# First loads of a normalization kernel split by even and odd partitions over two DMA queues

## The chip, the cores and the metric

The kernel runs on one core of one Trainium2 chip; the other cores are idle. The metric is the device time of one launch in microseconds (us). Comparisons are made with runs of the kernel before that were interleaved on the same chip. A program on one core can also have a run that is more than 1.5% above the fastest of the same kernel; such a run is called slow and is left out of the comparisons.

## The reference

```python
def reference(x, gamma):              # x: (4, 8, 16, 256, 256) f32, gamma: (8, 16) f32
    B, G, C_per_g, H, W = x.shape
    mu = x.mean(axis=(3, 4), keepdims=True)
    var = ((x - mu) ** 2).mean(axis=(3, 4), keepdims=True)
    x_norm = (x - mu) / np.sqrt(var + 1e-5)
    out = x_norm * gamma[None, :, :, None, None]
    return out.astype(np.float32)
```

Each of the 512 planes of 256 x 256 numbers is normalized by its own mean and variance and multiplied by one gamma. The input and the output are 134.22 MB each.

## The kernel before

The data are cut into 32 units of 4 MB. A unit is a tile of 128 partitions x 8192 f32, so one partition holds one row of 32 KB, and eight partitions hold one plane. Six tiles ("slots") are in SBUF. A unit is loaded, its sums are taken, it is normalized in place and stored; then the slot is loaded again.

```python
    AHEAD = 6
    slots = [data.tile([P, F], F32, name=f"xt{i}") for i in range(AHEAD)]

    def load(u, queue):
        queue.dma_start(out=slots[u % AHEAD][:], in_=xv[u])

    g_row = singles.tile([1, G * C], F32, name="g_row")
    for u in range(AHEAD):
        if u == 1:
            nc.scalar.dma_start(out=g_row[:], in_=gv[None, :])
        load(u, nc.scalar if u in (1, 3) else nc.sync)
    # ... constants, and gamma spread over the partitions ...
    for u in range(U):
        t = slots[u % AHEAD]
        nc.vector.reduce_sum(out=st[:, u, 0:1], in_=t[:], axis=AX.X)
        square = nc.scalar.activation(out=junk[:], in_=t[:], func=ACTF.Square, accum_out=st[:, u, 1:2])
        # ... matmul averages over 8 partitions; root, reciprocal, times gamma: scale ...
        nc.vector.tensor_scalar(out=t[:], in0=t[:], scalar1=ps[:, 0:1], scalar2=scale[:, u : u + 1],
                                op0=ALU.add, op1=ALU.mult)
        nc.scalar.dma_start(out=ov[u], in_=t[:])
        if u + AHEAD < U:
            load(u + AHEAD, nc.sync)
```

There are two DMA queues: that of SyncE (SP, shown as q1) takes loads only; that of ScalarE (ACT, shown as q10) takes units 1 and 3, gamma, and all stores. Both run on the same 16 DMA engines (each transfer leaves 16 completion packets in the trace, one for each engine). Below, "ring" is the line of transfers that wait in a queue. With gamma's row that makes 65 transfers. They use eight DMA semaphores in turn, so the last transfer, the 65th, is on the first semaphore again.

## Time and profile before

| | before |
|---|---|
| median, in the rounds with the changed kernel | 627.1 us (626.81 to 627.21, 4 runs) |
| span of the profiled run | 625.2 us |
| busiest compute engine | VectorE, 71% |
| two DMA queues together | 99.6% of the time of 16 engines |
| rows of 32 KB for each DMA engine | 512, at 1.21 us |

First the bytes moved, from the page: the span in 40 equal slices of 15.6 us.

```profile
GB/s 369 436 417 424 434 436 436 436 436 437 434 436 434 426 426 430 434 436 436 436 434 434 436 434 434 430 426 430 434 436 436 436 432 434 436 436 434 426 426 365
```

The rate stays between 426 and 437 but for the first slice, which holds the start, slices 3 and 4, in which the first store begins, and the last slice. Next come lines from the timeline: start in us, length in us, engine, line, operation; in brackets the idle time before and what ended it. They are the first reduce, and the issues of the first and second store.

```profile
20.32 8.69 DVE L103 TENSOR_REDUCE st<-xt 128x1 f32<-128x8192 f32 x1 [13.70 <-DMA xt<-in_x_dram]
...
35.38 0.35 ACTq L130 DMA_DIRECT2D out_dram<-xt  x1
...
50.30 0.35 ACTq L130 DMA_DIRECT2D out_dram<-xt  x1
```

VectorE starts on unit 0 only at 20.32 us, when the whole of it has landed. The change is aimed at this wait and at the following lines, the closing waits of SyncE (line view in the stretch 624.05 to 624.3 us: count, shortest/median/longest in ns, first start and last end in us):

```profile
L158 SPq EVENT_SEMAPHORE  x4: 28/28/38760, 585.3 to 624.2; - x4
L158 SPq DRAIN  x1: 7/7/7, 624.3 to 624.3; - x1
```

One wait of 38,760 ns holds the last landing, and three short ones stand behind it, ahead of the drain.

### The profile page before, as it was taken

How to read it: one execution, taken by the hardware profiler on the slowest of the kernel's cores; microseconds unless marked ns; L12 is line 12 of the kernel's file. 1: busy time of each engine (PE TensorE's matmuls, PEld its weight loads, DVE VectorE, ACT ScalarE, POOL GpSimd, SP SyncE). 2: the span in 40 equal slices, each digit the busy share in tenths (PEclk: the TensorE clock that was granted, in tenths of full speed). 3: DMA queues.
4: the chain of work that ended last, by engine and by line, in shares of the span. 5: the costliest groups of instructions: out<-in, count | busy, mean ns of one | idle time of the engine just before them, and what ended most of it. 6: DMA issues, size and time to landing. Idle time of an engine off the chain costs nothing.

```text
span 625.2 us, 626 instructions
## 1 busy us (share of the span) xinstructions
PE 21.4 (3%) x80; PEld 19.5 (3%) x80; DVE 443.2 (71%) x162; ACT 238.8 (38%) x98; POOL 1.3 (0%) x9
## 2 busy tenths in 40 slices
PE   2000000000000000000000000000000000000000
PEld 2000000000000000000000000000000000000000
DVE  0699999998867668676687766776667867668620
ACT  0444444444444224443244432344423443224400
POOL 0000000000000000000000000000000000000000
DMA  8999999999999999999999999999999999999998
GB/s 369 436 417 424 434 436 436 436 436 437 434 436 434 426 426 430 434 436 436 436 434 434 436 434 434 430 426 430 434 436 436 436 432 434 436 436 434 426 426 365
DMA packets 9220, 268.46 MB, mean 429 GB/s; under 512 B 1025, under 2 KB 1026, under 8 KB 1026
## 3 DMA queue, kind: packets, MB, share of 16 engines
q10 hardware_dynamic: 4898, 142.61, 52.8%
q1 hardware_dynamic: 4320, 125.83, 46.8%
q14 instruction: 2, 0.02, 0.0%
HBM read 134.22 MB, written 134.22 MB: 429 GB/s over the span
## 4 chain that ended last, share of the span: by engine, by line
another core or an unknown queue 64%; DMA 16%; DVE 13%; SPq 1%; PE 1%; issue 0%; ACT 0%
DMA xt<-in_x_dram 9%; DVE st L103 8%; DMA out_dram<-xt 7%; DVE xt L126 4%; SPq L48 1%; PE ps L112 1%; ACT std L117 0%; DVE nvar L113 0%; DVE rstd L121 0%; DVE scale L123 0%
## 5 line engine op out<-in xcount | busy, mean ns | idle before, releaser
L103 DVE TENSOR_REDUCE st<-xt 128x1 f32<-128x8192 f32 x32 | 277.9, 8684 | 111.2 <-DMA xt<-in_x_dram 111.2
L104 ACT ACTIVATE junk<-xt 128x8192 uint8<-128x8192 f32 x32 | 225.0, 7030 | 272.2 <-DMA xt<-in_x_dram 229.0
L126 DVE TENSOR_SCALAR xt<-xt,ps,scale 128x8192 f32<-128x8192 f32 x32 | 145.6, 4550 | 1.2
L117 ACT ACTIVATE std<-nvar,eps_t 128x1 f32<-128x1 f32 x32 | 9.4, 294 | 79.6 <-DVE nvar L113 79.6
L112 PE MATMUL ps<-st,navg 128*128 128x2 f32 x64 | 17.9, 349 | 568.0 <-DVE st L103 568.0
L112 PEld LDWEIGHTS ps<-st,navg 128*128 128x128 f32 x64 | 16.0, 312 | 569.8 <-issue 569.8
L113 DVE TENSOR_SCALAR nvar<-ps 128x1 f32<-128x1 f32 x32 | 9.2, 287 | 23.8 <-PE ps L112 23.8
L121 DVE RECIPROCAL rstd<-std 128x1 f32<-128x1 f32 x32 | 5.3, 164 | 11.6 <-ACT std L117 11.6
L104 ACT ACTIVATION_READ_ACCUMULATOR junk<-xt 128x1 f32 x32 | 6.0, 186 | 0.0
L123 DVE TENSOR_TENSOR scale<-rstd,g_col 128x1 f32<-128x1 f32 x32 | 5.1, 159 | 1.1
L84 PE MATMUL g_ps<-one,g_rep 1*128 1x1 f32 x16 | 3.5, 346 | 2.9 <-DVE g_rep L79 2.9
L84 PEld LDWEIGHTS g_ps<-one,g_rep 1*128 1x128 f32 x16 | 3.5, 325 | 2.9 <-POOL navg L68 2.9
L90 DVE COPY g_col<-g_ps 128x8 f32<-128x8 f32 x1 | 0.2, 166 | 3.7 <-PE g_ps L84 3.7
L74 ACT ACT_TABLE_LOAD x1 | 1.3, 1283 | 2.2 <-issue 2.2
L79 DVE COPY g_rep<-g_row 1x1024 f32<-1x1024 f32 x1 | 0.7, 681 | 2.1 <-DMA g_row<-in_gamma_dram 2.1
L64 POOL TENSOR_SCALAR_AFFINE_SELECT navg<-navg 128x128 f32<-128x128 f32 x1 | 0.4, 403 | 0.1
L68 POOL TENSOR_SCALAR_AFFINE_SELECT navg<-navg 128x128 f32<-128x128 f32 x1 | 0.4, 398 | 0.1
L63 POOL MEMSET navg<- 128x128 f32 x1 | 0.2, 220 | 0.0
L74 ACT ACTIVATE root_eps<-eps_t 128x1 f32<-128x1 f32 x1 | 0.2, 203 | 0.0
L147 POOL MEMSET const-bfloat16-1.0<- 128x1 bf16 x1 | 0.1, 101 | 0.0
L147 POOL MEMSET const-uint8-127<- 128x1 uint8 x1 | 0.1, 101 | 0.0
L147 POOL MEMSET const-float32-0.0<- 128x1 f32 x1 | 0.1, 98 | 0.3 <-issue 0.3
(3 smaller groups left out, 0.3 us busy)
## 6 DMA issues: line engine op xcount, KB each, us to landing
out_dram<-xt ACTq DMA_DIRECT2D x32, 4096.0 KB, 67.1
xt<-in_x_dram SPq DMA_DIRECT2D x30, 4096.0 KB, 33.8
xt<-in_x_dram ACTq DMA_DIRECT2D x2, 4096.0 KB, 33.3
g_row<-in_gamma_dram ACTq DMA_DIRECT2D x1, 0.5 KB
```

Of the source, the lines that this page charges most:

```text
L48: queue.dma_start(out=slots[u % AHEAD][:], in_=xv[u])
L74: nc.scalar.activation(out=root_eps[:], in_=eps_t[:], func=ACTF.Sqrt)
L79: nc.vector.tensor_copy(out=g_rep[:], in_=g_row[:].rearrange("o (n k) -> o n k", n=NG).unsqueeze(3).to_broadcast([1, NG, K, S]),)
L84: nc.tensor.matmul(out=g_ps[:, n : n + 1], lhsT=g_rep[:, n].rearrange("o k s -> o (k s)"), rhs=one[:], start=True, stop=True,)
L103: nc.vector.reduce_sum(out=st[:, u, 0:1], in_=t[:], axis=AX.X)
L104: square = nc.scalar.activation(out=junk[:], in_=t[:], func=ACTF.Square, accum_out=st[:, u, 1:2],)
L112: nc.tensor.matmul(out=ps[:], lhsT=navg_w, rhs=st[:, u], start=True, stop=True)
L113: nc.vector.tensor_scalar(out=nvar[:, u : u + 1], in0=ps[:, 0:1], scalar1=ps[:, 0:1], scalar2=ps[:, 1:2], op0=ALU.mult, op1=ALU.add,)
L117: nc.scalar.activation(out=std[:, u : u + 1], in_=nvar[:, u : u + 1], func=ACTF.Sqrt, bias=eps_t[:], scale=-1.0,)
L121: nc.vector.reciprocal(out=rstd[:, u : u + 1], in_=std[:, u : u + 1])
L123: nc.vector.tensor_mul(out=scale[:, u : u + 1], in0=rstd[:, u : u + 1], in1=g_col[:, g : g + 1],)
L126: nc.vector.tensor_scalar(out=t[:], in0=t[:], scalar1=ps[:, 0:1], scalar2=scale[:, u : u + 1], op0=ALU.add, op1=ALU.mult,)
```

## The change

The intent, as the diff reads, is to give VectorE its first unit earlier, by loading unit 0 through both queues at once, in half-tiles of every second partition, which by the formula for the SBUF ports (cited in the prediction) still reach all 16 ports. Units 1 to 6 are split as well, which makes 72 transfers, a multiple of eight, so that the last store is on the eighth semaphore, the last that the closing waits look at.

```diff
@@ -44,15 +44,23 @@
-    def load(u, queue):
-        queue.dma_start(out=slots[u % AHEAD][:], in_=xv[u])
+    def load(u, queue, rows=slice(None)):
+        queue.dma_start(out=slots[u % AHEAD][rows], in_=xv[u, rows])
+
+    even, odd = slice(0, P, 2), slice(1, P, 2)
 
 
     g_row = singles.tile([1, G * C], F32, name="g_row")
-    for u in range(AHEAD):
-        if u == 1:
-            nc.scalar.dma_start(out=g_row[:], in_=gv[None, :])
-        load(u, nc.scalar if u in (1, 3) else nc.sync)
+    load(0, nc.sync, even)
+    nc.scalar.dma_start(out=g_row[:], in_=gv[None, :])
+    load(0, nc.scalar, odd)
+    load(2, nc.sync, even)
+    for rows in (even, odd):
+        load(1, nc.scalar, rows)
+    load(2, nc.scalar, odd)
+    for u in range(3, AHEAD):
+        for rows in (even, odd):
+            load(u, nc.sync, rows)
@@ -129,7 +137,9 @@
         nc.scalar.dma_start(out=ov[u], in_=t[:])
         if u + AHEAD < U:
-            load(u + AHEAD, nc.sync)
+
+            for rows in (even, odd) if u == 0 else (slice(None),):
+                load(u + AHEAD, nc.sync, rows)
```

## The prediction

> **What bounds the kernel now.** I read the page first: its busy slices, its DMA queues, its groups, then the chain, then stretches of time.
>
> ```profile
> span 625.2 us, 626 instructions
> ...
> DVE  0699999998867668676687766776667867668620
> ACT  0444444444444224443244432344423443224400
> ...
> DMA  8999999999999999999999999999999999999998
> ...
> q10 hardware_dynamic: 4898, 142.61, 52.8%
> q1 hardware_dynamic: 4320, 125.83, 46.8%
> ...
> L103 DVE TENSOR_REDUCE st<-xt 128x1 f32<-128x8192 f32 x32 | 277.9, 8684 | 111.2 <-DMA xt<-in_x_dram 111.2
> ```
>
> The reader is to see that no compute engine is full (VectorE is the busiest at 71%, and it waits for loads), while the DMA row is full from the first slice to the last. The two queues together took 52.8 + 46.8 = 99.6% of the time of 16 engines. The data are 134.22 MB in and 134.22 MB out, in rows of 32 KB (one partition of a tile): 2 x 4096 rows, 512 for each DMA engine. 0.996 x 625.2 us / 512 = 1.216 us a row, which is the whole span. So the kernel is 512 row times, plus what stands before the first and after the last row.
>
> The chain of waits, in the middle, says the same:
>
> ```profile
> 161.81 0.33 SPq L48
> 162.14 18.96 another core or an unknown queue
> 181.09 0.02 SPq L48
> ...
> 181.15 0.33 SPq L48
> 181.47 18.96 another core or an unknown queue
> ```
>
> The load queue issues one load each 181.15 - 161.81 = 19.34 us. In that time one load and one store move, 8.39 MB, which is 434 GB/s; 16 rows an engine, 1.21 us each. One unit of compute is shorter: from its reduce at 20.32 to its store's issue at 35.38 is 15.06 us. Stretches of time (each row: stretch, its length, busy time of the engines, clock, DMA share, GB/s) show where the rate is missed:
>
> ```profile
> 21.36:40.72 19.36, 0.56 (x2) 0.50 (x2) 18.18 (x6) 11.32 (x4) 0.00 (x0) 1.00 1.00 433
> 40.72:60.08 19.36, 1.11 (x4) 1.00 (x4) 17.25 (x7) 9.74 (x6) 0.00 (x0) 1.00 0.98 408
> ...
> 300.00:319.36 19.36, 0.56 (x2) 0.50 (x2) 13.85 (x6) 7.42 (x3) 0.00 (x0) 1.00 1.00 433
> ```
>
> Steady pace is 433 already in the stretch in which only loads run (21 to 41 us), so loads alone are no faster and no slower than loads beside stores. One stretch is short: (433 - 408) / 433 x 19.36 = 1.1 us by this count, about 0.6 us of it real, since whole rows are counted where they fall. It is where the first store's rows begin to move. The rest is the ends: the first row starts about 1.8 us into the span, and the last rows end between 622 and 624 us, after which the last landing is seen and the program closes down by 625.2 us. Nothing else is lost.
>
> ```profile
> SPq L158 <- DMA out_dram<-xt: 41.1, 1, 41.1
> ```
>
> This line (the load queue's own waits) is the closing wait on line 158: a list of waits for the eight DMA semaphores, two at a time. The last store is there on the first semaphore, which the third of these waits names. Looked at by its times, that wait starts at 585.3 us and takes 38,760 ns, to 624.06 us, and three more waits come behind it before the closing drain at 624.3 us.
>
> **What the skill says.** DMA: Bandwidth & Descriptors, section "Issuing engines are not separate DMA queues": transfers issued by different engines run on the same 16 DMA engines and interleave, so issuing from two saves sequencer time only. The trace agrees: 433 GB/s while the scalar queue carries loads and while it carries stores. Same page, "Queues, rings and completion order": an engine goes round-robin between the queues that have work, at packet granularity. The trace agrees: unit 0 on one queue and unit 1 on the other land at 20.3 and 25.2 us, although 4 MB alone is 9.7 us at 433 GB/s. Same page, "Rules for kernel authors": two transfers to disjoint partition halves are not worth it, as they serialize on the same engines. SBUF — State Buffer, section "Door 1: The DMA port swizzle": 64 neighbouring partitions reach only 8 of 16 ports; by the formula given there even partitions alone, and odd ones alone, reach all 16. No transfer of 64 partitions is in the trace of before, so neither is tested by it.
>
> **The change, part by part.**
>
> *Bytes and rows.* The same 8192 rows of 32 KB; a transfer of 64 rows gives 4 rows to each of 16 engines if it spreads over all of them. Seven more transfers add seven semaphore writes to each engine, 4-byte packets. The 64 before cost nothing that can be seen: 16 rows fill the whole 19.36 us period including two such writes. So 0.
>
> *Unit 0 over both queues.* The queue of loads has a lead of three rows (u1 lands 4.9 us after u0, four row times, in an alternation that alone would give one). The fourth row of the scalar queue is then the tenth of the engine, and ends near 2.7 + 10 x 1.21 = 14.8 us, landing at 15.4 us. Unit 0 is ready 4.9 us earlier, and its store is issued at 30.5 us in place of 35.38. But the scalar queue carries the same 8 MB of loads as before (half 0, 1, half 2 for 1 and 3), until about 44 us, and the store's rows stand behind them in that ring. So the store's data start at 44 us and land at 64 us as before, and the load that waits for this store is issued as before.
>
> *Unit 1.* It now lies behind half of unit 0: its last row is the twelfth of the scalar queue, the 26th of the engine, 2.7 + 26 x 1.21 = 34.2 us, landing at 34.8 in place of 25.2. VectorE, done with unit 0 at 30.5, waits 4.3 us. The store of unit 1 comes at 34.8 + 15.06 = 49.9, before at 50.30. The gain on the compute side is 0.4 us by then, and stores still queue in a ring that is full. Worth 0.
>
> *New waits.* There are eight semaphores; the ninth transfer must wait until the first on its semaphore has landed. In the built program the second half of unit 2 waits for gamma's row (landed by 2.1 us), the halves of 4 and 5 for those of 0, 1 and 3, the first store for a half of unit 2, which lands near 24 us. The load ring holds three more halves, 6 MB, when the first of these waits ends, so no engine runs dry. 0 on the path.
>
> *First issue.* The first load takes 0.37 us to issue for 128 rows. A 64-row one could take less or more; every shift of the first row shifts the end, as nothing later has slack. The spread of issue times in the trace is 0.33 to 0.53 us, so I put this at +0.1, give or take 0.2 us.
>
> *Closing waits.* With 72 transfers the last store is on the eighth semaphore, which the last of the waits names. Three waits at about 0.06 us each stood behind the landing, from 624.06 to the drain at 624.29; all but one step goes: -0.12 us.
>
> Sum: 627.14 + 0 + 0.1 - 0.12 = 627.1 us. What the earlier start wins is on VectorE, which has 29% idle time.
>
> **The rivals.** (1) Halves collide on the SBUF ports. If an engine takes four neighbouring rows of a half, it writes two ports in turn, and two engines may write the same port at once while another rests. The seven split units are 7 x 8 = 56 rows an engine; at up to twice 1.21 us a row that is up to +68 us, 695 us. For it: 433 GB/s is the same for reads from and writes to HBM, as a limit on the SBUF side would have it. Against: engines need not march in step, and someone who needs 72 transfers would hardly pick splits that cost 10 us each. A partial collision of 10% would be +7 us. Together some 8%. (2) The ring runs dry: if a half lands later than I think, the new waits hold up the load queue at about 40 us. A hole of one row is 1.2 us an engine. The 6 MB in the ring speak against it; 628 to 630 us. (3) The start gains: the small loss at the first store (0.6 us) or the slow first row goes away when stores begin behind another mix of loads. 626.3 us. Nothing in the profile says that it must.
>
> **Range and chances.** The repeats of before lie within 0.16 us, so the range is that of the model: a few tenths either way for the start, the first store and which engine ends last, and some more above for small collisions or a dry ring: 626.2 to 628.4 us. Faster by over 2% would need 614.6 us; 512 rows at 1.21 us are 620 us, before start and end: 1%. Slower by over 2% (639.7 us) takes rival 1: 6%. The same: 93%.
>
> **What would show it.** Right: DMA queues again at 99 to 100% of the span, 433 GB/s in the stretch from 21 to 41 us, in which only halves and whole loads run; first reduce near 15 us, first store's issue near 30 us, second store's issue within 1 us of 50; load issues 19.34 us apart from 162 us on; the closing wait followed by one step to the drain. Wrong: below 430 GB/s before 41 us (ports), a stretch between 40 and 80 us with a DMA share clearly under that of before (dry ring), or a first row well away from 1.8 us.

## The result, and the profile after

| | before | after |
|---|---|---|
| median of 4 runs each | 627.1 us (626.81 to 627.21) | 628.0 us (627.63 to 628.14) |
| ratio | | 1.0014, interval 0.9997 to 1.0032 |
| span of the profiled run | 625.2 us | 626.0 us |
| first reduce starts | 20.32 us | 15.77 us |
| last store seen landed | 624.04 us | 625.06 us |

A ratio is the mean time of one kernel's fast runs over that of the other's fast runs of the same rounds, so it is not quite the ratio of the medians quoted beside it. The verdict is "the same" (within 2%): 0.9 us longer by the medians. The same file was run again later (below): ratio 1.002, interval 1.0008 to 1.0032, and all five of its runs took longer than all eleven of the kernel before. So the small loss is real, though this first comparison alone would not show it.

These are the page's lines for the changed kernel: the span, busy tenths and GB/s in 40 slices, the two DMA queues, the reduce on VectorE, and the half-tile loads with their median time from issue to landing.

```profile
span 626.0 us, 646 instructions
...
DVE  0869999988676687666776767867668676686730
...
DMA  8999999999999999999999999999999999999998
GB/s 369 436 402 435 435 436 435 433 432 431 429 426 431 433 435 435 433 435 435 435 431 435 433 433 431 431 427 431 433 435 433 433 435 435 433 435 435 433 433 345
...
q10 hardware_dynamic: 4930, 142.61, 52.8%
q1 hardware_dynamic: 4400, 125.83, 46.8%
...
L111 DVE TENSOR_REDUCE st<-xt 128x1 f32<-128x8192 f32 x32 | 277.9, 8684 | 114.7 <-DMA xt<-in_x_dram 114.7
...
xt<-in_x_dram SPq DMA_DIRECT2D x10, 2048.0 KB, 37.1
xt<-in_x_dram ACTq DMA_DIRECT2D x4, 2048.0 KB, 23.4
```

The two queues take the same share as before, so there is no hole of note between the rows. VectorE's total wait for loads is not shorter, 114.7 us in place of 111.2. The bytes differ in the third slice (402 in place of 417) and in the last (345 in place of 365). That is where to look.

What was meant to happen did happen. From the timeline of the changed kernel: the first reduce, the first store's issue, the second reduce, the second store's issue.

```profile
15.77 8.69 DVE L111 TENSOR_REDUCE st<-xt 128x1 f32<-128x8192 f32 x1 [9.16 <-DMA xt<-in_x_dram]
...
30.83 0.39 ACTq L138 DMA_DIRECT2D out_dram<-xt  x1
...
35.19 8.69 DVE L111 TENSOR_REDUCE st<-xt 128x1 f32<-128x8192 f32 x1 [4.39 <-DMA xt<-in_x_dram]
...
50.25 0.34 ACTq L138 DMA_DIRECT2D out_dram<-xt  x1
```

Unit 0 is ready 4.55 us earlier and its store is issued as much earlier. Unit 1 pays for it: VectorE waits 4.39 us for it, and by the second store the lead is 0.05 us. Even the first store has its lead in the ring only: its data land at 63.8 us, before at 64.4 us. The stretches of time that the prediction showed for before read in the changed kernel (length, busy time of the engines, clock, DMA share, GB/s):

```profile
21.36:40.72 19.36, 0.56 (x2) 0.50 (x2) 13.79 (x6) 7.36 (x4) 0.00 (x0) 1.00 1.00 433
40.72:60.08 19.36, 1.11 (x4) 1.00 (x4) 17.20 (x7) 9.21 (x6) 0.00 (x0) 1.00 0.99 408
300.00:319.36 19.36, 0.56 (x2) 0.50 (x2) 13.88 (x6) 7.44 (x4) 0.00 (x0) 1.00 1.00 433
```

The rates are 433, 408 and 433, as before: this count of whole rows is too coarse to show what moved. The chain of waits shows the steady pace, one load issue each 179.42 - 160.08 = 19.34 us:

```profile
160.08 0.33 SPq L48
160.41 18.96 another core or an unknown queue
...
179.42 0.33 SPq L48
```

The closing waits of SyncE after (line view, 615.5 to 625.3 us) are shorter, as meant: one short wait, then the drain.

```profile
L168 SPq EVENT_SEMAPHORE  x1: 28/28/28, 625.1 to 625.1; - x1
L168 SPq DRAIN  x2: 7/7/7, 625.1 to 625.2; - x2
```

SyncE's own waits (total us, times, longest us) hold the new ones: four waits of a load's issue for an earlier load.

```profile
SPq L48 <- DMA xt<-in_x_dram: 25.3, 4, 9.2
```

They lie where the ring is full, and cost nothing that the DMA share would show.

So where is the time lost? The first place is the first instruction. In the view of the tile, in the first 1.1 us, this is the issue of the first load (length in ns, then start in us), first before and then after:

```profile
L48 SPq DMA_DIRECT2D xt<-in_x_dram x1: 371/371/371, 0.8 to 0.8; - x1
```

```profile
L48 SPq DMA_DIRECT2D xt<-in_x_dram x1: 562/562/562, 0.8 to 0.8; - x1
```

The issue of 64 alternate partitions takes 0.19 us longer than that of all 128. The DMA view of the stretch 1.5 to 3.5 us, in slices of 0.05 us, shows the first rows start; again before, then after:

```profile
DMA  0000009990999000000900090000000000000000
```

```profile
DMA  0000000000000999909009000900909009000000
```

The first row starts in the slice at 1.80 us before and at 2.15 us after.

The second place is the first store. In the DMA view of 40 to 47 us, in slices of 0.175 us, 16 rows start about together, then nothing until they are through 1.21 us (7 slices) later. Before, then after:

```profile
DMA  9994004999000499900009990000000499000089
```

```profile
DMA  0099800009940005995000009999500000499400
```

Before, two row times from the group at the 14th slice to that at the 32nd take 18 slices in place of 14. After, from the 16th to the 35th, they take 19. I call this delay the stumble: the rows of the first store begin here, and the engines lose time once. In the row records of 30 to 60 us it is rows of the load queue that grow longer: 21 of them before and 32 after take over 1.27 us, up to 1.93 and 2.00 us, in place of 1.213; no store row does.

The third place is the end. In the DMA view of 619 to 627 us, in slices of 0.2 us, digits mark where rows start (the single digit far right is no row). Before, then after:

```profile
DMA  3970903970903990900000000000000000020000
```

```profile
DMA  3039997039997039993333000000000000000200
```

Before, the last rows start in the slice at 622.2 us, in tight groups. After, the groups are drawn out, and a few engines (the row of 3s) start their last rows as late as 623.2 us. All the data are moved when the last engine is through, not the mean one.

From the starts and ends of all rows in the two traces this account can be worked out. It splits the growth of the span, 626.03 - 625.17 = 0.86 us:

| term | before | after | difference |
|---|---|---|---|
| mean end of the engines' first row | 3.93 us | 4.23 us | +0.30 |
| delay at the first store's rows (the stumble) | 0.62 us | 0.86 us | +0.23 |
| everything else until the mean end of the last rows (623.06, 623.70 us) | | | +0.11 |
| last engine behind the mean one at its last row | 0.52 us | 0.91 us | +0.38 |
| from the last row's end to the landing that the program sees | 0.46 us | 0.45 us | -0.01 |
| from that landing to the end of the span | 1.13 us | 0.97 us | -0.16 |

The figures are rounded; the sum is +0.85 us.

When does the last engine fall behind? The completion packets of the transfers tell. Before, the last engine is 0.22 us behind the mean until 136 us, 0.58 us at 175 us and 0.52 us at the end. After, it is 0.28 us behind at 101 us, when the last half-tile has landed, 0.69 us at 140 us, 0.61 us at 411 us and 0.90 us at the end. The step in the middle comes with an instruction fetch, which the page of both kernels counts:

```profile
q14 instruction: 2, 0.02, 0.0%
```

The first of the two, a packet of 8 KB, runs at 155.8 us before and at 126.1 us after, for 0.31 us, and a data row that starts as it ends takes 1.56 us and 1.75 us in place of 1.213. The rest of the lag after, some 0.3 us, comes from 411 us on, when every transfer is whole. So little of the lag arose while the half-tiles ran: 0.06 us more than before, and 0.20 us in the second profile (e12, 0.42 us at 101 us).

### The profile page after: what moved, and what is told of

Its sections match the earlier page's. It is cut to its first block, busy times and chain, and to the rows that moved or that the text cites. A ratio compares the mean times of both kernels' runs of the same rounds, so it can differ in the third digit from the quotient of the medians.

```text
span 626.0 us, 646 instructions
## 1 busy us (share of the span) xinstructions
PE 21.4 (3%) x80; PEld 19.5 (3%) x80; DVE 443.4 (71%) x162; ACT 238.8 (38%) x98; POOL 1.3 (0%) x9
## 4 chain that ended last, share of the span: by engine, by line
another core or an unknown queue 64%; DMA 19%; DVE 9%; issue 2%; SPq 1%; PE 0%; ACTq 0%; ACT 0%; DVEq 0%
DMA xt<-in_x_dram 11%; DMA out_dram<-xt 7%; DVE st L111 7%; DVE xt L134 1%; SPq L48 1%; PE ps L120 0%; ACT std L125 0%; DVE nvar L121 0%; ACTq L48 0%; DVE rstd L129 0%; DVE scale L131 0%; ACTq L55 0%; DVEq L111 0%
## 5 line engine op out<-in xcount | busy, mean ns | idle before, releaser
L111 DVE TENSOR_REDUCE st<-xt 128x1 f32<-128x8192 f32 x32 | 277.9, 8684 | 114.7 <-DMA xt<-in_x_dram 114.7
```

## The experiments

Twelve kernels ran, each beside runs of the kernel before on the same chip (medians of it: 627.0, 627.01 and 626.77 us). All gave correct results. "Spread" below is how far the last of the 16 engines is behind the first at one and the same transfer, worked out from the times at which the engines' parts of it land in the trace; it was 0.9 us at the end of the kernel before and 1.35 us at the end of the changed one. Theories to be told apart: that the loss is in the first half-tile's issue; that the ports of SBUF collide; that transfers in halves make the DMA engines fall out of step.

### The first issue: whole, halves, columns

**e1_first_whole**: the change with unit 0 whole on one queue; unit 7 is split in its place, so that there are 72 transfers again.

```diff
-    load(0, nc.sync, even)
+    load(0, nc.sync)
     nc.scalar.dma_start(out=g_row[:], in_=gv[None, :])
-    load(0, nc.scalar, odd)
...
-            for rows in (even, odd) if u == 0 else (slice(None),):
+            for rows in (even, odd) if u in (0, 1) else (slice(None),):
```

> The change, but unit 0 is loaded whole by the load queue, and unit 7 is split in its place, so that there are still 72 transfers and the last store is on the eighth semaphore. Start theory (the first issue of a half takes 0.56 us where a whole tile took 0.37, and the first row comes 0.3 us later): issue back at 0.37 us, first row back at 1.8 us, time about 0.3 us under the change, 627.7 us. First-store theory (most of the loss is a larger stumble at 42 to 46 us, where the first store's rows meet halves in the load ring): first row back, but the stumble stays and the time stays within 0.1 us of the change. If both are real: 627.7 us with the larger stumble still there.

Measured: fast runs from 627.16 to 631.47 us, one slow run of 640.07; ratio 1.005 (1.0031 to 1.007). The expected start came, as the view of the tile and the DMA view of 1.5 to 3.5 us show for this kernel:

```profile
L48 SPq DMA_DIRECT2D xt<-in_x_dram x1: 378/378/378, 0.8 to 0.8; - x1
```

```profile
DMA  0000009999990090000090900009000000000000
```

The expected time did not. In the profiled run (629.65 us) the spread is 0.6 us at the start, 2.75 us at 114 us, about when the split loads of unit 7 go by, and 4.3 us at 577 us; that last growth falls in a stretch of whole loads. One engine ends late. This was not in any theory when the run was sent, and it made the spread the second question.

**e3_first_halves**: the kernel before with unit 0 alone in two halves, both on SyncE's queue (66 transfers).

```diff
-        load(u, nc.scalar if u in (1, 3) else nc.sync)
+        for rows in (even, odd) if u == 0 else (slice(None),):
+            load(u, nc.scalar if u in (1, 3) else nc.sync, rows)
```

> The kernel before, with unit 0 alone split by even and odd partitions, both halves on the load queue: 66 transfers, last store on the second semaphore. Start theory: first issue 0.56 us, first row near 2.15 us, 0.3 us slower than before, 627.4 us. If the later first row of the change came from the order of the two queues and not from the half: first row stays at 1.8 us and the time at 627.1 us.

Measured: 627.4 us (627.3 to 627.97), ratio 1.001 (0.9998 to 1.0023), so 0.4 us above before, as expected. Issue and first rows (same two views):

```profile
L48 SPq DMA_DIRECT2D xt<-in_x_dram x1: 557/557/557, 0.8 to 0.8; - x1
```

```profile
DMA  0000000000009999999000900900000090000000
```

Both stand where the changed kernel has them. With 378 ns in e1 this shows that the longer issue belongs to the half-tile of 64 partitions and to nothing else in the change. The same view of e4 below reads 560 ns, so it is the number of 64 partitions and not their being alternate.

**e5_columns**: the change with halves by columns: all 128 partitions, 16 KB of each row.

```diff
-        queue.dma_start(out=slots[u % AHEAD][rows], in_=xv[u, rows])
+        queue.dma_start(out=slots[u % AHEAD][:, rows], in_=xv[u, :, rows])
 
-    even, odd = slice(0, P, 2), slice(1, P, 2)
+    even, odd = slice(0, F // 2), slice(F // 2, F)
```

> The change, with its halves cut by columns (all 128 partitions, 16 KB of each row) in place of partitions: the same order, queues and 72 transfers, but rows of half the size. Start theory in its narrow form (a transfer of 64 partitions is slower to issue): issue back near 0.37 us, first row near 1.8 us. If any half is slower to issue: 0.56 us again. Port theory (rows of partition halves collide when engines are out of step): no collision here, last slice of the page back at 365 GB/s, time 626.9 to 627.1 us with the closing gain of 0.15 us. If smaller rows cost by themselves, 112 rows of 16 KB an engine at even 20 ns each would add 2 us.

Measured: 627.79 us (627.37 to 628.13), ratio 1.0011 (0.9998 to 1.0023); 0.7 to 0.9 us above what was expected. The issue is short again (0.37 us) and the first row starts at 1.80 us, but the stumble is about 1 us and the spread 1.1 us. So half a tile by itself is not slow to issue; half the partitions are. The larger stumble costs some 0.3 us of the gain. The smaller rows cost more: a row of 16 KB took 0.611 us (median, 60 to 120 us), two of them 9 ns more than one row of 32 KB, which over 56 row pairs an engine is an estimated 0.5 us.

### The ports

**e4_blocks**: the change with halves of neighbouring partitions, 0 to 63 and 64 to 127.

```diff
-    even, odd = slice(0, P, 2), slice(1, P, 2)
+    even, odd = slice(0, P // 2), slice(P // 2, P)
```

> The change, with halves of neighbouring partitions (0 to 63 and 64 to 127) in place of even and odd ones. Port theory of the skill's table (64 neighbouring partitions reach 8 of 16 ports): each half runs at about half the rate where no transfer of the other half is beside it, so the seven split units cost up to 56 rows of 1.21 us an engine, 68 us more, some 640 to 695 us, and reduce of unit 0 starts later than 15 us. If the spread over engines alone decides: within 0.3 us of the change, 628.0 us.

Measured: 687.48 us (684.83 to 690.86), ratio 1.0968 (1.0941 to 1.0994). The page:

```profile
span 683.1 us, 646 instructions
...
DMA  9999999999999999999999999999999999999997
GB/s 203 203 209 213 215 292 313 363 413 437 430 430 432 436 434 434 432 430 437 432 432 432 439 434 434 430 432 436 432 430 434 437 434 436 430 434 434 432 430 305
```

The engines are as busy as ever, but rows take 2.39 to 2.58 us (20 to 85 us) and the rate is halved for five slices of 17.1 us. The Trainium skill's page SBUF — State Buffer, section "Door 1: The DMA port swizzle", gives 64 neighbouring partitions 8 of the 16 ports; the same page's section "Can I just issue two DMAs to hit both halves?" says that two transfers at once do not make up for it. Both agree with 203 to 215 GB/s here, while half-tiles were under way on two queues. The even and odd halves of the changed kernel kept 433 GB/s. A loss of the size that the first rival of the prediction gave (+68 us at most) is thus real for blocks of neighbours, and the change's way of cutting avoids it.

### Halves in the middle of the run

**e2_mid_halves**: the kernel before with units 12 to 18 split, in place of units 0 to 6 (72 transfers). It leaves the start alone.

```diff
-            load(u + AHEAD, nc.sync)
+            for rows in (even, odd) if 12 <= u + AHEAD < 19 else (slice(None),):
+                load(u + AHEAD, nc.sync, rows)
```

> The kernel before, with the loads of units 12 to 18 alone split by even and odd partitions, in mid-run, so that there are 72 transfers and the last store is on the eighth semaphore, while start and first store are as before. If halves cost nothing in themselves: first row at 1.8 us, stumble as before, closing 0.12 to 0.16 us shorter, 627.0 us. Port theory (rows of halves are slower): rate in the stretch of the split loads under 433 GB/s, up to several us more. A mid-run fee of 0.1 us, as the change shows over its first 100 us, would just cancel the closing gain: 627.1 us.

Measured: 632.82 us (632.72 to 635.68), ratio 1.0107 (1.0092 to 1.0122). It was expected to cost nothing, and cost 5.8 us. The page of the run:

```profile
GB/s 368 432 430 432 432 432 432 432 432 433 432 432 432 432 432 431 432 428 430 395 434 432 434 432 432 432 432 434 441 432 432 432 438 432 434 432 432 436 432 251
```

The last slice is at 251 where before had 365: some engines are done while others still work. The spread is 0.81 us at 200 us, when the split loads begin, 5.3 us at 363 us, soon after the last of them, and 5.4 us from there to the end: it grows while they run. The row records show how. From 195 to 370 us 88 rows, of loads and of stores, took over 1.27 us, up to 2.59 us in place of 1.213, 28 us in all; in the kernel before only 2 of the 6911 rows after 100 us did.

**e8_all_halves**: all units of the kernel before split by even and odd.

```diff
-        load(u, nc.scalar if u in (1, 3) else nc.sync)
+        for rows in (even, odd):
+            load(u, nc.scalar if u in (1, 3) else nc.sync, rows)
...
-            load(u + AHEAD, nc.sync)
+            for rows in (even, odd):
+                load(u + AHEAD, nc.sync, rows)
```

> The kernel before, with the loads of all units split by even and odd partitions. Seven split units in mid-run cost 5.8 us. Mixture theory (rows collide only while some engines write rows of a half and others those of a whole tile): little mixing here, time under 629 us. Out-of-step theory (a half's rows collide whenever engines are out of step): engines fall apart further the longer it lasts, 32 split units cost 10 us or more, and the last slice of the page falls well under 250 GB/s.

Measured: 654.35 us (653.85 to 658.09), ratio 1.0447 (1.0423 to 1.0472). The page:

```profile
DMA  9999999999999999999999999999999999999666
GB/s 377 421 415 439 423 443 417 443 415 401 434 429 432 427 431 417 429 425 423 425 429 409 421 423 423 419 411 411 431 419 405 420 395 424 405 405 401 292 278 264
```

In the last three slices the DMA share is 6 tenths: a part of the engines has nothing left. The spread stays under 0.5 us up to 101 us and grows to 38 us by 525 us. After 100 us 508 rows took over 1.27 us, up to 3.0 us. So a mixture of whole and half loads (a theory after e1 and e2) is not needed; halves alone do it, and the more of them the more.

**e9_skew_before** and **e10_skew_change**: four extra transfers, into a tile that nobody reads, put one engine about 5 us behind the others from the start, in the kernel before and in the changed one. They ask whether being out of step is itself what costs.

```diff
+    skew = singles.tile([P, 480], F32, name="skew")
+    for i in range(4):
+        r = slice(17 * i, 17 * i + 17)
+        (nc.sync, nc.scalar)[i % 2].dma_start(out=skew[r], in_=xv[U - 1, r, :480])
```

> The kernel before, with four small transfers of 17 rows of 1920 B each put ahead of all others, two on each of the two queues, into a tile that nothing reads. 17 rows go to one DMA engine alone, so one engine starts some 130 KB behind the others, about 5 us at its pace, and has that much more to do. Whole tiles only. Out-of-step theory: an engine behind the others does no harm beyond its own extra work where all transfers are whole: 5 to 6 us more, 632 to 633 us. If being out of step harms whole tiles too: 637 us or more.

> The change with the same four small transfers ahead of all others. Out-of-step theory: the engine that is behind now runs through the split units out of step, its rows collide with those of others, and the time grows by clearly more than in the kernel before: 5 us of its own and at least 3 us more, 636 us or over. If halves do no harm by being out of step, and what cost 5.8 us in mid-run was something else there (the mix with stores, the waits for semaphores): the same 5 to 6 us as in the kernel before, 633 to 634 us.

Measured: e9 631.4 us (631.16 to 632.22), ratio 1.0076 (1.0061 to 1.0091); e10 635.81 us (634.4 to 638.28), ratio 1.0147 (1.0129 to 1.0164). The lines of bytes, first e9, then e10:

```profile
GB/s 333 427 433 433 433 433 433 433 433 432 433 433 432 431 435 435 435 433 433 433 433 433 433 433 433 433 433 433 433 433 433 433 433 433 433 433 433 433 433 281
```

```profile
GB/s 329 432 430 430 430 430 428 430 437 432 434 441 432 430 430 432 432 430 438 432 434 440 432 430 430 432 432 432 434 436 432 440 434 430 430 432 430 432 430 182
```

In e9, with whole loads, the spread of the stores' queue stays at 6.25 us from 33 to 575 us: the engine that is behind stays as far behind and costs that time once, as the flat 433 shows. In e10 it is 7.7 us at first, 8.8 at 111 us, when the last half-tile has landed, 10.6 from 229 us on, and the last slice falls to 182. The difference of the two medians is 4.4 us, of which the change itself accounts for 0.9 to 1.4. So the same small transfers cost more in the changed kernel. Not shown is that the half-tiles do it alone, since most of the growth falls after them, among whole loads.

**e11_mid_columns**: e2 with halves by columns, each of which covers all partitions.

```diff
-        queue.dma_start(out=slots[u % AHEAD][rows], in_=xv[u, rows])
+        queue.dma_start(out=slots[u % AHEAD][:, cols], in_=xv[u, :, cols])
...
-            for rows in (even, odd) if 12 <= u + AHEAD < 19 else (slice(None),):
-                load(u + AHEAD, nc.sync, rows)
+            for cols in (left, right) if 12 <= u + AHEAD < 19 else (slice(None),):
+                load(u + AHEAD, nc.sync, cols)
```

> The run with units 12 to 18 split in mid-run, with the halves cut by columns in place of partitions: the same 72 transfers, waits and order, but every row of every transfer goes to the port that it goes to in a whole tile. Port theory: no engine falls behind, 626.8 to 627.3 us. If splitting in itself (more transfers, more semaphore waits, slower supply of descriptors) made engines fall behind: near 632 us as with partition halves.

Measured: the fast runs took 630.35 to 636.6 us, ratio 1.0089 (1.0059 to 1.0119); two of six were slow (645.34, which is the profiled one, and 651.58). Its profile is thus of a slow run, and only the growth of the spread is read from it: 1.0 us at 210 us, 3.4 at 225, 8 at 350 us, when the split loads are through, up to 18 later. Column halves touch every partition just as a whole load does, yet here too an engine falls behind, and the fast runs, of which there is no profile, are 0.9% longer. Collisions that come of which partitions an engine writes (my explanation of e2 at that point) are therefore not needed for the loss. The columns also halve the rows to 16 KB, so this run does not tell whether partition halves lose time for the same reason. Why a split load in mid-run makes single rows longer and drives the engines apart is left open.

### Smaller ones

**e6_gamma_pool**: the kernel before with gamma's row issued by GpSimd, which leaves 64 transfers on the two queues, so that the closing gain comes alone.

```diff
-            nc.scalar.dma_start(out=g_row[:], in_=gv[None, :])
+            nc.gpsimd.dma_start(out=g_row[:], in_=gv[None, :])
```

> The kernel before, with gamma's row loaded through the Pool queue: nothing split, and 64 transfers on the eight semaphores, so that the last store is on the eighth. If the closing gain is what it seems (three waits behind the landing become one): closing 0.15 us shorter, 626.85 us. If the Pool's transfer brings a wait of its own at the close or a later start: 627.0 us or more.

Measured: 627.21 us (626.72 to 627.43), ratio 1.0 (0.9987 to 1.0014). The closing is shorter (last landing seen at 624.73, drain at 624.81 us), but the spread of this run is 1.5 us (it jumps from 0.53 to 1.66 at about 160 us, where an instruction fetch stands at 156.4 us), and no gain is seen. Its last engine ends 1.08 us behind the mean, more than in the changed kernel, though no load is split.

**e7_sync_only**: the kernel before with all loads on SyncE's queue. It asks whether the stumble comes of stores that stand behind loads in ScalarE's ring.

```diff
-        load(u, nc.scalar if u in (1, 3) else nc.sync)
+        load(u, nc.sync)
```

> The kernel before, with all loads on the load queue, so that the first store stands behind no load in its own queue: reduce of unit 0 starts near 12 us and the first store's rows move from 27 us on. If the stumble is the price of the first store's rows whenever they come: a stretch short by some 0.6 us, now near 27 us instead of 44, time 627.0 us. If it is the price of a queue that turns from loads to stores: no stumble, 626.4 us.

Measured: 627.54 us (627.27 to 629.41), ratio 1.0013 (1.0 to 1.0026). The first reduce is at 13.2 us and the first store is issued at 28.25. The stumble moves forward with the store, to between 33 and 45 us, and it is larger, about 1.3 us. So it belongs to the first store's rows, wherever they come, and an even earlier first store gains nothing either. Its profiled run is the slowest of the five (629.41 us): the spread grows from 0.6 us at 23 us to 4.7 us at 94 us and is 3.0 us at the end. Here too no load is split, so whole loads can drive the engines apart as well, around the first stores.

**e12_change_again**: the change, without any edit. It asks whether the late last engine of the first profile was chance.

> The change once more, unedited, for a second profile. Systematic parts should come back: first issue 0.56 us, first row near 2.15 us, closing 0.15 us shorter than before. The part that I take for chance, how far the last engine ends behind the mean of all (0.4 us worse in the first profile), may differ: 627.4 to 628.2 us.

Measured: 628.13 us (628.0 to 628.2, 5 runs), ratio 1.002 (1.0008 to 1.0032). The first issue and the DMA view of 619 to 627 us:

```profile
L48 SPq DMA_DIRECT2D xt<-in_x_dram x1: 551/551/551, 0.8 to 0.8; - x1
```

```profile
DMA  9037999037999037999030300000000000000300
```

The issue is long again, and again a few engines start their last rows late, here up to 623.4 us. The spread is 1.43 us at the end, the closing 0.97 us. By the completion packets the last engine is 0.56 us behind the mean at 411 us and 0.91 us at the end, so the late growth comes again. The loss of the changed kernel thus repeats in its terms. Of the kernel before there is one profile only, and e6, with whole loads alone, has a later last engine; how much of the difference in this term is the change's is therefore not shown.

None of the twelve was faster than the kernel before, and no version that beats both came out of them. A start with the first load whole and later halves (e1) would save some 0.3 us (an estimate from the mean end of the first row) and loses more where its spread grows.

## Why the prediction was right or wrong

**What bounds the kernel: right.** The two queues' share is the same after as before to the tenth of a per cent, and no run in which compute began earlier (the change, e7) was faster than before.

**Unit 0 earlier, worth nothing: right.** Predicted 15.4 us for the first reduce and 30.5 for the first store's issue; seen 15.77 and 30.83. The difference is the late first row, below. Landing of this store: 64 us predicted, 63.8 seen.

**Unit 1 later, worth nothing: right.** Predicted 34.8 us for its landing and 49.9 for its store; seen 35.1 and 50.25.

**New waits, worth nothing: right.** SyncE has four of them, and the rows go on without a hole.

**Closing, -0.12 us: right.** It was -0.16 us in the change, and e12 has the same closing.

**First issue, +0.1: the mechanism was right, and the size was off.** It measured +0.30 us at the mean first row, at the edge of the give-or-take of 0.2. The first row at 2.15 us is also one of the signs that the prediction had named as wrong ("well away from 1.8 us"). I had taken the spread of issue times of whole tiles for that of half tiles; e3, e4 and e12 show 0.55 to 0.56 us for 64 partitions, and e1 and e5 0.37 to 0.38 for 128.

**First store, 0: mis-sized.** The third rival took up "the small loss at the first store (0.6 us)" and supposed that it might go away. It grew by 0.23 us. It varies with the mix of loads that the store meets (0.62 before, 0.75 in e3, about 1.0 in e5, about 1.3 in e7), and what makes rows longer there is open.

**"Which engine ends last": the missing term.** The prediction named it only as a part of the range, "a few tenths either way", and left it out of the sum. It is +0.38 us, the largest term, and the changed kernel's late engine came back in e12. That split loads in mid-run drive engines apart, by single rows that take longer, is shown by e2 and e8. That they did so in the change is not shown: when its last half-tile has landed, at 101 us, the last engine is 0.28 us behind the mean (0.42 in e12), before 0.22. Both kernels then step up at an instruction fetch, and the changed one gains its further 0.3 us from 411 us on, among whole loads; why is open.

**The rivals.** A loss at the ports (1) did not show in the change, and e4 shows what another cut costs: 60 us against +68 at most. The ring did not run dry (2). The start gained nothing (3). The measured 628.0 us is in the range of 626.2 to 628.4, at its upper part; the 0.9 us above the predicted 627.1 is the three terms above, 0.20 + 0.23 + 0.38 us beyond what was put down for them, with 0.1 us of other delay. That the earlier start would win nothing was foreseen with its reason; the direction of these small terms was not.

## What to carry to other kernels

Where the DMA engines are full from end to end, as here, an earlier start of compute is worth nothing: only the first row's start, delays of the rows between, the last engine's last row and the closing can move the time, so look at these four by their rows. Keep loads whole in the steady part of such a kernel: splitting seven of 32 loads there cost 5.8 us and splitting all of them 27 us, while the number of bytes and the digits of the DMA share in the middle looked as before. If a tile must be cut, do not cut it into partitions 0 to 63 and 64 to 127 (60 us here, against 0.9 us for alternate partitions and 0.8 us for columns at the same places), and read the last slice of the GB/s row for engines that fell behind. Before a late engine is put down to a change, look at when it fell behind: here an instruction fetch and a stretch far from the change did part of it.

## What the Trainium skill lacked or had wrong

- DMA: Bandwidth & Descriptors, "Rules for kernel authors", says of two transfers to disjoint partition halves that they are not worth it. That holds, but its reason (they share the same engines) would make them neutral. Here they cost: 5.8 us for seven split loads in mid-run (e2) and 27 us for all 32 (e8), because single rows take longer, up to 3.0 us in place of 1.213, and the engines drift apart, by up to 40 us. Halves by columns do it too (e11, ratio 1.0089). No section that I read has this.
- SBUF — State Buffer, "Can I just issue two DMAs to hit both halves?", speaks of blocks at partitions 0 and 64 only, and these it has right (203 to 215 GB/s in e4). It concludes that one transfer over all 128 partitions is the only way to all ports. Two transfers of alternate partitions moved 433 GB/s here (21 to 41 us of the changed kernel).
- DMA: Bandwidth & Descriptors, "Issuing engines are not separate DMA queues", calls the issuing time usually small. At the very start it counts in full, and it depends on the shape: 0.55 to 0.56 us for 64 partitions, alternate or neighbouring (e4), 0.37 to 0.38 us for 128 partitions, whether whole rows or half rows.
- No page that I read has the delay when a first store meets running loads: 0.62 us in the kernel before, up to about 1.3 us in e7.
- No page that I read has what an instruction fetch costs the data rows of a full DMA engine: its packet of 8 KB takes 0.31 us, and the data row that starts as it ends 1.56 us before and 1.75 us after in place of 1.213.
